# Fourth pass of an FFN's inner products: each matrix's two halves in one load, gate with two tiles and up with three

## The chip, the cores and the metric

The kernel runs on one core of a Trainium2 chip. The metric is the device time of one execution in microseconds, and less is better. Five engines work side by side, each with its own queue of instructions: TensorE (PE, with PEld for weight loads), VectorE (DVE), ScalarE (ACT), GpSimd (POOL) and SyncE (SP), which here issues nearly all DMAs. An instruction waits at the head of its engine's queue until its inputs are there and the buffer that it writes is free; whatever stands behind it on that engine waits too.

## The reference

One block of a network on a sequence of 2048 tokens of width 1024: a mixer of stick-breaking attention and causal pooling, and then a dense feed-forward part, which is where the change lies:

```python
h = rmsnorm(x, g_ffn_pre[l]) * (1.0 + scale_f) + shift_f
f = (jax.nn.silu(h @ w_gate[l]) * (h @ w_up[l])) @ w_down[l]
x = x + gate_f * rmsnorm(f, g_ffn_post[l])
```

`w_gate` and `w_up` are 1024 x 2816, `w_down` is 2816 x 1024, all in f32.

## The kernel before, in words

The three products of the feed-forward part are done by a fast matrix scheme of seven products instead of eight (Strassen's, in Winograd's form), on two levels. The outer level splits tokens, width and the 22 column blocks of 128 into halves. Some of its products are done first, in four passes, `p1` to `p4`; each pass again uses the seven-product scheme. A pass has 11 columns `j`, a column has seven steps, and a step is two pairs of operands, each multiplied in three matmuls (every f32 operand is split into a high and a low part, and high x high, high x low and low x high are added). After the four passes the main stage begins, whose first column is `gate_up(0)`.

A column of a pass is made by `inner(q, j)`; `m = 11 q + j` counts columns, so the fourth pass is `q == 3`, `m` from 33 to 43. Its parts:

- `load()`: the weights of the column into raw tiles. In passes one to three that is a tile with a 256 KB block of gate and one of up. In the fourth pass the operands are the sums of the two halves of the weights' rows, so four blocks come: `g`, `g2`, `u`, `u2nd`.
- `row_sum` (fourth pass alone): POOL adds `g2` into `g`, and `u2nd` into `u`.
- `s12` and `s34`: POOL makes the scheme's four sums of the blocks of `g` and `u`, in tiles `s`.
- `split_w` in each step: ACT makes the high part and its rounded copy, DVE subtracts for the low part (L1177), into operand tiles `w` for PE. The seven steps take `g`, `s12`, `s12`, `g`, `s34`, `u`, `s34`, and their banks are called `a`, `e`, `f`, `b`, `h`, `i`, `d`; in the trace they are `ap`, `ep` and so on.
- `take_*` and `done`: DVE adds the banks up; a finished partial sum lies in a tile `p_c` of tag `s`, which has six buffers, and is stored by SP to DRAM (`pd`) two steps later. The main stage loads it again (`px`).

The order is set by a list of steps. Each step carries work for earlier steps, with the number of steps ahead:

```python
r[0].ahead = [({1: 9, 2: 12}.get(m, 16 if q == 3 else 14), load), (5 if m == 1 else 8, s12), (4 if m == 1 else 7, s34)]
if q == 3:
    r[0].ahead += [(10, lambda: row_sum("g", "g2")), (9, lambda: row_sum("u", "u2nd"))]
```

So a column's loads are asked for 16 steps ahead, its row sums 10 and 9, `s12` 8 and `s34` 7. On PE, ACT, DVE and POOL the instructions run in this order. SP's queue is ordered by a scheduler that places each DMA by when it reckons its tile free and its data ready; that order is fixed at build time.

Between the steps POOL also adds up the token operands of later products: `hs` tiles, loaded by SP (L1617) from DRAM and added by POOL (L1687).

Raw tiles come from two pools, `fx` and `ring`, each with one buffer per tag: `w320` and `w321` in either, and `gf` in `fx`; all hold two blocks of 256 KB (`cu`, of two buffers, holds one block each). The fourth pass before: the first halves of gate and up in one tile, which goes around three places (`fx` `w321`, `ring` `w320`, `fx` `w320`); the second halves of both in another, which goes around two (`ring` `w321`, `gf`).

Of the kernel before, what the change touches and what calls it, by code (L numbers as in the profile page):

```python
# [17 lines left out]
P = 128  # L18
# [3 lines left out]
HK = KC // 2  # L22
# [6 lines left out]
TB = 512  # L29
# [10 lines left out]
NQ = 4  # L40
# [7 lines left out]
def block_kernel(ctx, tc, x, c, w_cond, b_cond, g_mix_pre, g_mix_post, w_in, w_pool,  # L48
                 pool_scale, w_out, g_ffn_pre, g_ffn_post, w_gate, w_up, w_down, out):
    nc = tc.nc  # L50
# [3 lines left out]
    w_gate, w_up, w_down = w_gate[0], w_up[0], w_down[0]  # L54
# [10 lines left out]
    def rows(w):  # L65
        return w.rearrange("(kc p) n -> p kc n", p=P)

    def mm3(ps, terms, first=True, last=True):

        n = len(terms)  # L70
        for i, ((lh, ll), (rh, rl)) in enumerate(terms):
            nc.tensor.matmul(ps, lh, rh, start=first and i == 0, stop=False)  # L72
            nc.tensor.matmul(ps, lh, rl, start=False, stop=False)  # L73
            nc.tensor.matmul(ps, ll, rh, start=False, stop=last and i == n - 1)  # L74

    def open_pool(stack, name, bufs=1, side=None):
        kw = {"side": side} if side else {}
        return stack.enter_context(tc.tile_pool(name=name, bufs=bufs, reuse_waits="tile", **kw))
# [39 lines left out]
    def ft(tag, name, shape=(P, TB)):  # L118
        return fx.tile(list(shape), F32, tag=tag, bufs=FT[tag], name=name)
# [980 lines left out]
    for n in range(len(steps) + OFF):  # L1100
# [4 lines left out]
        if n < len(steps):  # L1105
            u, i = steps[n]
# [6 lines left out]
        if n >= OFF:  # L1113
            u, b = steps[n - OFF]
# [37 lines left out]
    ring = open_pool(ctx, "ring", bufs=RB)  # L1152
    SBT = S // 2
    NTS = SBT // P
    HF = NF // 2
# [3 lines left out]
    def operand(name, pool=None):  # L1159
        if pool is None:  # L1160
            used[0] += 1
            pool = fx if fx is not None and used[0] % (RB + 1) == 0 else ring
        return [pool.tile([P, TB], F32R, tag=f"w{n}", bufs=1 if pool is fx else RB, name=f"{name}_{n}") for n in "hl"]

    def split_by_bank(hi, lo, src):

        if low_ps is None:
            return split(hi, lo, src)
        nc.scalar.copy(hi, src)
        n = 1  # L1170
        for d in src.shape[1:]:
            n *= d
        both = low_ps("rounded")[:, 0:n]
        if len(src.shape) == 3:
            both = both.rearrange("p (a b) -> p a b", a=src.shape[1])
        nc.scalar.copy(both, raw(hi))
        nc.vector.tensor_tensor(lo, src, both, ALU.subtract)  # L1177
# [123 lines left out]
    def raw_tile(pool, n, name, shape):  # L1301
        tag = f"w32{int(n)}"
        return ft(tag, f"{name}_32{int(n)}", shape) if pool is fx else pool.tile(list(shape), F32, tag=tag, bufs=1, name=f"{name}_32{int(n)}")

    def raw_pair(pool, name, shape):
        return [raw_tile(pool, n, name, shape) for n in range(2)]

    def later(steps_on, do):
        takes.setdefault(n + steps_on, []).append(do)

    def rows_of(src, k0, f):
        return rows(src)[:, k0:k0 + HK, f * P:(f + 1) * P]

    def inner(q, j):

        p = f"p{q + 1}"
        name = f"{p}_{j}"
        m = HF * q + j
        st = {}

        def load():
            if m == 0:
                st["g"], st["u"], st["s12"], st["s34"] = (t[:, n] for t in raw_pair(ring, name, (P, 2, TB)) for n in range(2))
            else:
                turn = 0 if m == 1 else (31 - m) % 4
                pool, n = ((fx, 1), (ring, 0), (fx, 0))[m % 3] if m >= 30 else (ring if turn > 1 else fx, turn % 2 == 0)
                w = ft("gf", f"{name}_32", (P, 2, TB)) if m == NQ * HF - 1 else raw_tile(pool, n, name, (P, 2, TB))
                st["g"], st["u"] = w[:, 0], w[:, 1]
            k0, f = ((0, j), (HK, j), (HK, j + HF), (0, j + HF))[q]
            parts = [("g", w_gate, k0), ("u", w_up, k0)]  # L1330
            if q == 3:
                if m == NQ * HF - 2:
                    st["g2"], st["u2nd"] = (ft("cu", f"{name}_2{n}") for n in "gu")
                else:
                    w = raw_tile(ring, 1, f"{name}_2", (P, 2, TB)) if m % 2 else ft("gf", f"{name}_2", (P, 2, TB))
                    st["g2"], st["u2nd"] = w[:, 0], w[:, 1]
                parts = [parts[0], ("g2", w_gate, HK), parts[1], ("u2nd", w_up, HK)]
            for n, src, k in parts:
                (nc.scalar if m in (4, 5) else nc.sync).dma_start(st[n].rearrange("p (k n) -> p k n", k=HK), rows_of(src, k, f))

        def row_sum(n, other):
            nc.gpsimd.tensor_tensor(st[n], st[n], st[other], ALU.add)

        half = TB // 2
        one, two = slice(0, half), slice(half, TB)

        def sum_tile(n):
            if n not in st:
                st[n] = ft("sr", f"{name}_{n}")
            return st[n]  # L1350

        def s12():
            t, g, u = sum_tile("s12"), st["g"], st["u"]
            nc.gpsimd.tensor_tensor(t[:, one], u[:, one], u[:, two], ALU.add)
            nc.gpsimd.tensor_tensor(t[:, two], t[:, one], g[:, one], ALU.subtract)

        def s34():
            t, g, u = sum_tile("s34"), st["g"], st["u"]
            nc.gpsimd.tensor_tensor(t[:, one], g[:, one], u[:, one], ALU.subtract)
            nc.gpsimd.tensor_tensor(t[:, two], g[:, two], st["s12"][:, two], ALU.subtract)  # L1360

        def step(w, part, v, vpart, bank, after, split_first=True):

            def split_w():
                if split_first:
                    pair = operand(f"{name}_{w}")
                    cols = two if w == "u" else slice(0, TB)
                    split_by_bank(*(t[:, cols] for t in pair), st[w][:, cols])
                    st[w + "r"] = [x.rearrange("p (k n) -> p k n", k=HK) for x in pair]

            def mm():
                st[bank] = (e_ps if bank in "de" else p_ps)(f"{bank}{name}")
                (wh, wl), (th, tl) = st[w + "r"], ys[p][v]
                mm3(st[bank], [((wh[:, 2 * part + k, :], wl[:, 2 * part + k, :]), (th[:, 2 * vpart + k, :], tl[:, 2 * vpart + k, :]))
                               for k in range(2)])

            return Step(1, split_w, mm, [(1, do) for do in after])

        def keep(kind, sb, t):
            nc.sync.dma_start(pd[sb][:, j, q // 2 * 4 + 2 * kind + q % 2, :], t)  # L1380

        def done(kind, sb, ps, rest):
            t = ft("s", f"{name}_c{kind}{sb}")
            nc.vector.tensor_tensor(t, ps, rest, ALU.add)
            later(2, lambda: keep(kind, sb, t))

        def take_p1():
            st["p1"] = ft("p1", f"p1{name}")
            nc.scalar.copy(st["p1"], st["a"])

        def take_p5():
            st["u4"] = t = ft("gf" if not q and m and m % 2 == 0 else "u4", f"u4{name}")
            if not q:
                nc.scalar.copy(t, st["e"])

        def take_p6():
            st["u2"] = ft("u2", f"u2{name}")
            nc.vector.tensor_tensor(st["u2"], st["f"], st["p1"], ALU.add)
            if q:
                nc.vector.tensor_tensor(st["u4"], st["e"], st["u2"], ALU.add)  # L1400
            else:
                nc.gpsimd.tensor_tensor(st["u4"], st["u4"], st["u2"], ALU.add)

        def take_p7():
            st["u3"] = ft("u3", f"u3{name}")
            nc.vector.tensor_tensor(st["u3"], st["h"], st["u2"], ALU.add)

        r = [step("g", 0, "ya", 0, "a", [take_p1]),
             step("s12", 0, "v14", 0, "e", [take_p5]),
             step("s12", 1, "v32", 1, "f", [take_p6], False),  # L1410
             step("g", 1, "ya", 1, "b", [lambda: done(0, 0, st["b"], st["p1"])], False),
             step("s34", 0, "v32", 0, "h", [take_p7, lambda: done(1, 1, st["e"], st["u3"])]),
             step("u", 1, "v14", 1, "i", [lambda: done(1, 0, st["i"], st["u3"])]),
             step("s34", 1, "y22", 0, "d", [lambda: done(0, 1, st["d"], st["u4"])], False)]
# [3 lines that stand above are left out]
        return r  # L1418
# [747 lines left out]
```

## Time and profile before

| what | us |
|---|---|
| median of three runs | 2224.97 |
| the runs | 2221.27, 2224.97, 2226.73 |
| the profiled execution, its time | 2223.88 |
| its span | 2222.1 |
| PE busy | 2179.7 |
| second pass, from the first matmul of its `ap` to that of the third | 105.76 |
| third pass, first eight columns | 76.16 |
| fourth pass, first ten columns (1305.64 to 1420.32) | 114.68 |

All views are of the profiled execution, and times in them are microseconds from its span's start. In the tables by stretch a cell is an engine's busy time and, after the x, its instructions. In a table of waits a row says which engine, at which line, waited for whom. In a timeline a row has its start, its length, engine, line, operation, `out<-in` by tile names without numbers, and in square brackets the idle time ahead of it with what ended it. All loads of the passes are called `p` in the trace (`p_s` the sums, `p_g_l`, `p_u_l`, `p_s_l` low parts).

### The profile page before, as it was taken

To read this page: it belongs to the slowest core of one execution; us is meant where nothing else is said; L and a number is where in the kernel's file an instruction comes from. 1 tells how busy PE (TensorE), PEld (TensorE's weight loads), DVE (VectorE), ACT (ScalarE), POOL (GpSimd) and SP (SyncE) were. 2 spreads that over 40 slices of the span, in tenths; PEclk is the share of its full clock that TensorE was granted. 3 is DMA by queue.
4 is the path that set the end of the run, shared out by engine and by line. 5 is a ranking of instruction groups with operands and counts; after the bars stand their busy time and mean duration, and the time that the engine had idled before them with its cause. 6 is when DMAs were issued, how large, how long until landed. Compare 5 with 4: busy or idle time off the path is not lost.

```text
span 2222.1 us, 34293 instructions
## 1 busy us (share of the span) xinstructions
PE 2179.7 (98%) x10349; PEld 1794.8 (81%) x10349; DVE 1673.5 (75%) x2552; ACT 1355.9 (61%) x2796; POOL 1215.6 (55%) x1700
## 2 busy tenths in 40 slices
PE   8999999999999999999999999899999999999998
PEld 6888888888888888878888877678888888888887
DVE  7874599999999966557777867697788775577566
ACT  5434599989889845447666655554444444455444
POOL 1452277787779965547888666556565520033003
PEclk9999999999999999999999999999999999999999
DMA  8996876534444456678899867899999897679553
GB/s 312 343 291 205 286 208 179 157 96 119 130 114 110 133 176 209 199 230 286 272 318 334 265 204 247 271 316 314 324 320 296 294 338 269 208 243 329 183 199 121
DMA packets 365909, 524.78 MB, mean 236 GB/s; under 512 B 24534, under 2 KB 204314, under 8 KB 358172
## 3 DMA queue, kind: packets, MB, share of 16 engines
q1 hardware_dynamic: 363164, 521.02, 71.7%
q8 instruction: 82, 1.34, 0.3%
q10 hardware_dynamic: 2560, 1.58, 0.2%
q14 instruction: 103, 0.84, 0.1%
HBM read 350.01 MB, written 172.49 MB: 235 GB/s over the span
## 4 chain that ended last, share of the span: by engine, by line
PE 77%; DVE 6%; DMA 5%; POOL 4%; issue 3%; ACT 3%; SPq 1%; DVEq 0%; POOLq 0%; ACTq 0%
PE wt L964 4%; PE dn0p L73 3%; PE dn0p L74 3%; PE dn0p L72 3%; PE dn1p L72 3%; PE dn1p L73 3%; PE dn1p L74 3%; PE av L980 2%; PE z L929 2%; PE z L930 2%; PE av L979 2%; DMA pd<-p_c 2%; PE mix L72 2%; PE mix L74 2%; PE mix L73 2%
## 5 line engine op out<-in xcount | busy, mean ns | idle before, releaser
L953 POOL TENSOR_TENSOR w<-sg,pr 128x512 f32<-128x512 f32 (+2 forms) x320 | 306.3, 957 | 46.4 <-DVE pr L948 14.7
L948 DVE TENSOR_TENSOR_SCAN pr<-pr,carry,begin 128x512 f32<-128x512 f32 x192 | 244.1, 1271 | 0.0
L932 ACT ACTIVATE sg<-z 128x512 f32<-128x512 f32 (+2 forms) x320 | 183.7, 574 | 50.9 <-PE z L930 40.2
L63 DVE TENSOR_TENSOR wtl<-wt,wth 128x512 fp32r<-128x512 f32 (+1 forms) x320 | 189.7, 593 | 17.8 <-ACT wth L62 15.6
L62 ACT CAST wth<-wt 128x512 fp32r<-128x512 f32 (+1 forms) x320 | 183.1, 572 | 10.4 <-PE wt L964 10.4
L934 ACT ACTIVATE pr<-z 128x512 f32<-128x512 f32 (+2 forms) x320 | 183.1, 572 | 0.0
L964 PE MATMUL wt<-ident,w 128*128 128x128 f32 x1088 | 172.3, 273 | 1.6 <-POOL pr L944 1.1
L964 PEld LDWEIGHTS wt<-ident,w 128*128 128x128 f32 x1088 | 134.1, 140 | 32.7 <-POOL pr L944 1.9
L1481 ACT ACTIVATE sa<-sa 128x512 f32<-128x512 f32 x88 | 54.7, 632 | 154.3 <-DVE sa L1480 147.4
L979 PE MATMUL av<-wth,vt 128*128 128x512 f32 (+1 forms) x320 | 126.2, 394 | 0.9 <-ACT o L984 0.8
L72 PE MATMUL dn0p<-w0p_h,g0p_h 128*128 128x512 f32 x308 | 119.8, 389 | 0.0
L73 PE MATMUL dn0p<-w0p_l,g0p_h 128*128 128x512 f32 x308 | 119.8, 389 | 0.0
L74 PE MATMUL dn0p<-w0p_h,g0p_l 128*128 128x512 f32 x308 | 119.8, 389 | 0.0
L929 PE MATMUL z<-kt,qt 128*128 128x512 f32 (+2 forms) x320 | 118.7, 371 | 0.7 <-ACT pr L934 0.6
L980 PE MATMUL av<-wtl,vt 128*128 128x512 f32 (+1 forms) x320 | 117.7, 368 | 1.3 <-DVE wtl L63 1.2
L63 DVE TENSOR_TENSOR g0p_l<-g0p,g0p_h 128x512 fp32r<-128x512 f32 x77 | 58.4, 759 | 79.5 <-ACT g0p_h L62 79.5
L930 PE MATMUL z<-kt,qt 128*128 128x512 f32 (+2 forms) x320 | 116.9, 365 | 0.0
L72 PE MATMUL dn1p<-w1p_h,g1p_h 128*128 128x512 f32 x292 | 113.6, 389 | 0.0
L73 PE MATMUL dn1p<-w1p_l,g1p_h 128*128 128x512 f32 x292 | 113.6, 389 | 0.0
L74 PE MATMUL dn1p<-w1p_h,g1p_l 128*128 128x512 f32 x292 | 113.6, 389 | 0.0
L945 DVE TENSOR_TENSOR_SCAN pr<-pr,zero,begin 128x128 f32<-128x128 f32 (+3 forms) x128 | 111.3, 871 | 1.7 <-ACT pr L934 1.7
L62 ACT CAST g0p_h<-g0p 128x512 fp32r<-128x512 f32 x77 | 48.0, 623 | 104.9 <-PE dn0p L73 90.9
(847 smaller groups left out, 7157.5 us busy)
## 6 DMA issues: line engine op xcount, KB each, us to landing
pd<-p_c SPq DMA_DIRECT2D x176, 256.0 KB, 4.9
px<-pd SPq DMA_DIRECT2D x42, 1024.0 KB, 8.6
hs<-h2d SPq DMA_DIRECT2D x78, 256.0 KB, 4.7
wc<-in_w_cond_dram SPq DMA_DIRECT2D x32, 512.0 KB, 7.6
qt<-qd SPq DMA_DIRECT2D x64, 256.0 KB, 4.1
p<-in_w_gate_dram SPq DMA_DIRECT2D x52, 256.0 KB, 4.9
p<-in_w_up_dram SPq DMA_DIRECT2D x52, 256.0 KB, 4.9
kt<-kd SPq DMA_DIRECT2D x96, 128.0 KB, 3.3
```

The costliest lines, as they stand in the source:

```text
L62: nc.scalar.copy(hi, src)
L63: low.tensor_tensor(lo, src, raw(hi), ALU.subtract)
L72: nc.tensor.matmul(ps, lh, rh, start=first and i == 0, stop=False)
L73: nc.tensor.matmul(ps, lh, rl, start=False, stop=False)
L74: nc.tensor.matmul(ps, ll, rh, start=False, stop=last and i == n - 1)
L929: nc.tensor.matmul(z[:, 0:L], qt[:, 0, i * P:(i + 1) * P], keys, start=True, stop=False)
L932: nc.scalar.activation(sg[:, 0:L], z[:, 0:L], AF.Sigmoid, scale=0.125)
L934: nc.scalar.activation(pr[:, 0:L], z[:, 0:L], AF.Sigmoid, scale=-0.125)
L948: nc.vector.tensor_tensor_scan(keys, keys, begin, carry, ALU.mult, ALU.bypass)
L953: nc.gpsimd.tensor_tensor(w[:, 0:L], sg[:, 0:L], pr[:, 1:L + 1], ALU.mult)
L964: nc.tensor.transpose(wt[:, i * P:(i + 1) * P], wss[u][i][:, b * P:(b + 1) * P], ident)
L979: nc.tensor.matmul(av[:, lo0:], vb, wh[:, lo0:], start=first, stop=False)
```

## The change

In the fourth pass both halves of one matrix come in one transfer of 512 KB into one tile, `[P, 2, TB]` with the first half in `[:, 0]`: up into the tile that held the first halves (three places), gate into the one that held the second halves (two places; odd columns `m` now in `gf`, even ones in `ring` `w321`). The last column, whose up goes into `gf`, has its gate in two `cu` tiles with two loads of 256 KB; before, two `cu` tiles were used in the column ahead of it. Up's load is asked for after gate's in the code. Row sums, differences, splits and matmuls are as before, and PE, ACT, DVE and POOL have the same instructions in the same order, apart from the tiles' names. SP has 21 DMAs fewer. The diff:

```diff
-            k0, f = ((0, j), (HK, j), (HK, j + HF), (0, j + HF))[q]
-            parts = [("g", w_gate, k0), ("u", w_up, k0)]
             if q == 3:
-                if m == NQ * HF - 2:
-                    st["g2"], st["u2nd"] = (ft("cu", f"{name}_2{n}") for n in "gu")
+                f = j + HF
+                if m == NQ * HF - 1:
+                    st["g"], st["g2"] = (ft("cu", f"{name}_{n}") for n in ("g", "g2"))
+                    for n, k in (("g", 0), ("g2", HK)):
+                        nc.sync.dma_start(st[n].rearrange("p (k n) -> p k n", k=HK), rows_of(w_gate, k, f))
                 else:
-                    w = raw_tile(ring, 1, f"{name}_2", (P, 2, TB)) if m % 2 else ft("gf", f"{name}_2", (P, 2, TB))
-                    st["g2"], st["u2nd"] = w[:, 0], w[:, 1]
-                parts = [parts[0], ("g2", w_gate, HK), parts[1], ("u2nd", w_up, HK)]
-            for n, src, k in parts:
-                (nc.scalar if m in (4, 5) else nc.sync).dma_start(st[n].rearrange("p (k n) -> p k n", k=HK), rows_of(src, k, f))
+                    v = ft("gf", f"{name}_g", (P, 2, TB)) if m % 2 else raw_tile(ring, 1, f"{name}_g", (P, 2, TB))
+                    st["g"], st["g2"] = v[:, 0], v[:, 1]
+                    nc.sync.dma_start(v.rearrange("p h (k n) -> p (h k) n", k=HK), rows(w_gate)[:, :, f * P:(f + 1) * P])
+                st["u"], st["u2nd"] = w[:, 0], w[:, 1]
+                nc.sync.dma_start(w.rearrange("p h (k n) -> p (h k) n", k=HK), rows(w_up)[:, :, f * P:(f + 1) * P])
+                return
+            k0, f = ((0, j), (HK, j), (HK, j + HF))[q]
+            for n, src in (("g", w_gate), ("u", w_up)):
+                (nc.scalar if m in (4, 5) else nc.sync).dma_start(st[n].rearrange("p (k n) -> p k n", k=HK), rows_of(src, k0, f))
```

SP's queue before, in the middle of the fourth pass. A name such as `p4_5_2` is pass 4, column 5, second halves; `p4_4_320` the first halves of column 4; `c00`, `c11`, `c10`, `c01` are a column's four partial sums:

```order
L1339 DMA p4_5_2_17376<-in_w_gate_dram 128x4x128
L1380 DMA pd0_158<-p4_0_c00_17138 128x512
L1339 DMA p4_5_2_17376<-in_w_up_dram 128x4x128
L1380 DMA pd1_159<-p4_0_c11_17152 128x512
L1380 DMA pd0_158<-p4_0_c10_17166 128x512
L1339 DMA p4_4_320_17248<-in_w_gate_dram 128x4x128
L1339 DMA p4_4_320_17248<-in_w_up_dram 128x4x128
L1617 DMA hs0_2_1_17338<-h2d6_126 128x512
L1380 DMA pd1_159<-p4_0_c01_17207 128x512
L1617 DMA hs0_2_3_17340<-h2d6_126 128x512
```

The same place after (lines are five further on):

```order
L1385 DMA pd0_158<-p4_0_c00_17130 128x512
L1385 DMA pd1_159<-p4_0_c11_17144 128x512
L1385 DMA pd0_158<-p4_0_c10_17158 128x512
L1340 DMA p4_4_320_17240<-in_w_up_dram 128x8x128
L1622 DMA hs0_2_1_17328<-h2d6_126 128x512
L1385 DMA pd1_159<-p4_0_c01_17199 128x512
L1338 DMA p4_4_g_17241<-in_w_gate_dram 128x8x128
L1622 DMA hs0_2_3_17330<-h2d6_126 128x512
L1385 DMA pd0_158<-p4_1_c00_17251 128x512
```

Before, the second halves of a column stood ahead of the first halves of the column before it; now a column's two loads stand together, after three and after four stores, and no load of a later column is ahead of them.

SP's queue before at the end of the pass, from the last loads of the pass to the main stage's first, `g_0`:

```order
L1339 DMA p4_9_321_17860<-in_w_up_dram 128x4x128
L1339 DMA p4_10_32_17979<-in_w_up_dram 128x4x128
L1339 DMA p4_10_2_321_17980<-in_w_up_dram 128x4x128
L1617 DMA hs8_0_1_18367<-h2d12_132 128x512
L1380 DMA pd0_158<-p4_6_c00_17874 128x512
L1617 DMA hs8_3_1_18097<-h2d15_135 128x512
L1380 DMA pd1_159<-p4_6_c11_17889 128x512
L1380 DMA pd0_158<-p4_6_c10_17906 128x512
L1617 DMA hs8_3_3_18099<-h2d15_135 128x512
L1440 DMA g_0_321_18013<-in_w_gate_dram 128x8x128
```

The same place after, from the stores of column 6 on:

```order
L1385 DMA pd0_158<-p4_6_c00_17853 128x512
L1385 DMA pd1_159<-p4_6_c11_17868 128x512
L1385 DMA pd0_158<-p4_6_c10_17885 128x512
L1622 DMA hs8_3_1_18076<-h2d15_135 128x512
L1622 DMA hs8_3_3_18078<-h2d15_135 128x512
L1445 DMA g_0_320_18010<-in_w_gate_dram 128x8x128
L1385 DMA pd1_159<-p4_6_c01_17923 128x512
L1340 DMA p4_10_32_17958<-in_w_up_dram 128x8x128
L1622 DMA hs8_0_1_18346<-h2d12_132 128x512
L1385 DMA pd0_158<-p4_7_c00_17971 128x512
```

The last column's up has moved behind a load of the main stage, `g_0_320`, and `g_0_321` has moved behind the stores of column 7.

## The prediction

> **What bounds the kernel now.** I read the page first: busy times, then the slices.
>
> ```profile
> span 2222.1 us, 34293 instructions
> PE 2179.7 (98%) x10349; PEld 1794.8 (81%) x10349; DVE 1673.5 (75%) x2552; ACT 1355.9 (61%) x2796; POOL 1215.6 (55%) x1700
> PE   8999999999999999999999999899999999999998
> DMA  8996876534444456678899867899999897679553
> ```
>
> TensorE (PE) is the bound, and only its pauses can be won. Most slices read 9. The one 8 inside the row is slice 26 of 40, near 1390 us, where the fourth pass runs. So the second view is a table of stretches, cut where a first matmul of a row `ap` starts: the second pass, the first eight columns of the third pass, its last three, ten columns of the fourth, its last column, and the first column of the main stage.
>
> ```profile
> core 0: us, PE busy (x) PEld busy (x) DVE busy (x) ACT busy (x) POOL busy (x), PEclk, DMA share, GB/s
> 1092.12:1197.88 105.76, 105.27 (x463) 86.57 (x462) 82.63 (x137) 68.61 (x131) 90.92 (x100) 1.00 0.93 313
> 1197.88:1274.04 76.16, 76.16 (x337) 63.08 (x336) 60.00 (x99) 50.90 (x98) 52.34 (x59) 1.00 0.84 277
> 1274.04:1305.64 31.60, 29.64 (x128) 23.34 (x126) 23.44 (x40) 17.54 (x34) 21.21 (x25) 1.00 0.73 245
> 1305.64:1420.32 114.68, 101.47 (x422) 78.17 (x420) 74.44 (x124) 62.78 (x118) 74.32 (x76) 0.99 0.71 226
> 1420.32:1431.99 11.67, 10.26 (x43) 7.49 (x42) 7.26 (x13) 4.69 (x9) 3.23 (x3) 1.00 0.82 270
> 1431.99:1468.25 36.26, 34.89 (x150) 28.08 (x151) 30.00 (x45) 23.53 (x41) 19.68 (x16) 1.00 0.99 345
> ```
>
> A column j is 42 matmuls (7 steps of 6). The second row shows eight columns in 76.16 us, PE never idle: 9.52 us each, at full clock. Ten columns of the fourth pass take 114.68 where that rate gives 95.2: 19.48 us lost, 1.95 a column. The stretch before loses 31.60 - 28.56 = 3.04, the last column 11.67 - 9.52 = 2.15. No other engine is full there: DVE works 7.44 us a column, POOL 7.43, ACT 6.28, and the DMA share, 0.71, is lower than in either pass before. So something waits in a ring. The waits of the ten columns, by engine:
>
> ```profile
> PE ep L72 <- DVE p_c L1384: 5.6, 4, 2.7
> PE ap L72 <- DVE u2p L1398: 4.2, 5, 1.9
> DVE p_c L1384 <- DMA pd<-p_c: 33.4, 13, 5.2
> ACT rounded L1176 <- DVE p_s_l L1177: 25.5, 9, 5.4
> SPq L1339 <- POOL p L1342: 32.8, 6, 7.0
> SPq L1617 <- POOL hs L1687: 14.2, 5, 6.1
> ```
>
> (us in total, times, longest.) Read backwards: PE waits for DVE, DVE for stores of partial sums (`pd`) to land so that a slot of `s` is free, and the stores stand in SP's queue, which is held 32.8 us at the loads of L1339 by POOL's row sums, L1342. Order of time shows it closing:
>
> ```profile
> 1317.94 1.29 POOL L1342 TENSOR_TENSOR p<-p,p 128x512 f32<-128x512 f32 x1 [1.30 <-DMA p<-in_w_up_dram]
> 1319.26 0.38 SPq L1339 DMA_DIRECT2D p<-in_w_gate_dram  x1
> 1323.78 0.58 SPq L1339 DMA_DIRECT2D p<-in_w_up_dram  x1
> 1327.44 1.27 POOL L1342 TENSOR_TENSOR p<-p,p 128x512 f32<-128x512 f32 x1 [2.69 <-DMA p<-in_w_gate_dram]
> 1328.87 1.29 POOL L1342 TENSOR_TENSOR p<-p,p 128x512 f32<-128x512 f32 x1 [0.16 <-DVE u2p L1398]
> 1330.19 0.38 SPq L1339 DMA_DIRECT2D p<-in_w_gate_dram  x1
> 1333.40 1.31 SPq L1339 DMA_DIRECT2D p<-in_w_up_dram  x1
> 1340.01 1.30 POOL L1342 TENSOR_TENSOR p<-p,p 128x512 f32<-128x512 f32 x1 [0.85 <-DMA p<-in_w_up_dram]
> 1341.33 0.38 SPq L1339 DMA_DIRECT2D p<-in_w_gate_dram  x1
> 1346.02 0.69 DVE L1384 TENSOR_TENSOR p_c<-ip,u3p 128x512 f32<-128x512 f32 x1 [2.67 <-DMA pd<-p_c]
> ```
>
> Up's row sum of a column ends at 1319.23; within 0.03 us SP issues the second-half load of the column two later, which needs the tile that this sum has just read. Behind it in the queue stand stores and, last, the first-half load (1323.78) that the next column's row sums need. It lands, the sums run (1327.44, 1328.87), and SP is let go again at 1330.19, then at 1341.33. One turn is 10.93 and 11.14 us, and gives one column, where PE needs 9.52. At 1346.02 DVE pays: its slot's store left SP only after 1341.33.
>
> **The change part by part.**
>
> *Taken away: the second-half tile that a row sum frees late.* A second half lived in a tile of two buffers; its load for column j+2 waited for the row sum of j, ahead of column j+1's first halves. Afterwards the row sum reads and writes inside one tile; nothing is freed at its end. That wait, 32.8 us on SP, has no instruction to hang on.
>
> *Added: the gate tile of two buffers.* It is freed by DVE's rest of the gate (L1177) and by the second difference `s34` (L1360), both of column j, and its load for j+2 waits for both. So a ring remains, but it gives two columns a turn and has 19.04 us for them. From `s34` to `s34`: issue 0.38, landing L, two row sums, two halves of `s12`, one head-sum (`hs`, L1687) between, two of `s34`. Durations and landings:
>
> ```profile
> 1330.24 0.73 POOL L1354 TENSOR_TENSOR p_s<-p 128x256 f32<-128x256 f32 x1
> 1344.30 1.28 POOL L1687 TENSOR_TENSOR hs<-hs,hs 128x512 f32<-128x512 f32 x1
> L1339 SPq DMA_DIRECT2D p<-in_w_up_dram x19: 425/491/1315, 1289.7 to 1394.9; - x19
> DMA to landing us min/median/max: 3.1/4.6/5.8
> ...
> L1440 SPq DMA_DIRECT2D g<-in_w_gate_dram x22: 383/384/3434, 1407.6 to 1728.8; - x22
> DMA to landing us min/median/max: 6.3/8.4/10.8
> ```
>
> That is 0.38 + L + 2.58 + 1.46 + 1.28 + 1.46 = L + 7.2. No load of 512 KB runs in this pass; bounds: L is at least the 4.6 us of a 256 KB load here, and at most the 10.8 us of a 512 KB load in the main stage. I take 8.4, the same size. The turn is then 15.6 us against 19.04, 3.4 to spare; with 10.8 it is 18.0 and still fits. Price 0, range 0 to 0. The cover is this slack; without it the next late thing is POOL's row sum and behind it the same p_c.
>
> The Trainium skill (DMA: Bandwidth & Descriptors, section Anatomy of one DMA) fits 2.0 us plus bytes over 436 GB/s, on GpSimd's path; for 512 KB an estimate of 3.2 us by that page. By it the turn would be 10.4 us and the sum below the same, with no chance left for the slow ring; the trace's 8.4 for that size says otherwise and is used.
>
> *Up's tile of three buffers* is freed by DVE a whole column earlier than needed; price 0, covered by that column's 9.52 us.
>
> *Loads merged: 4 issues a column become 2*, 21 fewer on SP. At 0.38 to 0.49 us each a column's SP work falls by about 0.9 us. SP is not full, so it is worth 0 to 9 us (ten columns), and I count it inside the ring above: 0.
>
> *Moved in SP's queue:* the gate load now stands behind a column's fourth store and ahead of two `hs` loads and the next column's stores. It passes no instruction on POOL, DVE, ACT or PE. While it waits for `s34` (POOL runs that one column ahead of PE), stores behind it are late. Price per column: between the second pass, where loads of both kinds share SP and a column loses (105.76 - 104.72)/11 = 0.09 us, and the stretch before the ring fills, 3.04/3 = 1.01. Ten columns: 0.9 to 10.1. POOL here has 7.43 us of work a column, less than the second pass's 8.27, and the DMA share is lower too, so I stay near the lower end: 3.3, about half of it the `hs` waits at L1617, which the change leaves.
>
> *The end of the pass.* The last column's gate goes into two tiles of another kind with two loads, and of the main stage's first loads one, `g_0_321`, moves behind five stores and one `hs` load. Price between -2.15 (its loss goes) and +2.72 (two steps more of PE); I take +0.5.
>
> *The stretch 1274 to 1305.* Its waits begin with an `hs` on POOL, which stays, and end in the ring: of 3.04 I take back 0.7.
>
> Sum: -(19.48 - 3.3) + 0.5 - 0.7 = -16.4 us, on the profiled execution's 2223.88: **2207.5, said as 2208**. That execution lies 1.1 us under the median of the three runs, 2224.97, which range over 5.5 us; about 0.3% (6.7 us) is what a measurement of this kernel can tell from no change.
>
> **The rivals.**
>
> *B, the pass at PE's rate.* The third pass shows that seven steps, their stores and `hs` loads fit when loads come in time. Both small terms vanish: 19.48 + 3.04 + 2.15 = 24.7, so 2199. Against: DVE must finish `u2p` just in time for `ap` (4.2 us in five waits), which is no load's fault.
>
> *C, the new place of the gate load holds SP.* If each gate load stands behind one `hs` wait of the longest kind, 6.1, the ring is 15.6 + 6.1 = 21.7 us for two columns, 10.85 each: ten columns in 108.5, a gain of 6.2, and 2217.7. At the mean, 14.2/5 = 2.8, it is 18.4 and costs nothing. I give half the gain lost, 2212 to 2218.
>
> *D, no real change.* PE's waits name DVE, none names a load. If DVE's chain rather than its stores set the pace, time stays 2224. Against: 33.4 us of DVE's idleness ends with a landing of `pd`.
>
> *E, slower: the ring of two columns turns too slowly.* It decides once L + 7.2 is over 22.94 (two columns of now), L over 15.8. With L = 20, ten columns take 136 us: +21, 2245. For it: 512 KB take nearly twice the time of 256 KB, and one buffer fewer stands behind gate. Against: no 512 KB load of the two tiles in the main stage took over 10.8, at a DMA share of 0.99.
>
> The Trainium skill (Perfetto Trace Analysis, section DMA Optimizations) says that where DMA engines are generally idle, splitting a transfer may let the work end sooner; the change merges instead, with the share at 0.71. By that rule E's case gains; that the row sum starts only when both halves are there, merged or not, speaks against it.
>
> **How the numbers follow.** A, as summed, 2204 to 2212: 0.60. B, 2199 to 2204: 0.14. C, 2212 to 2218: 0.15. D: 0.06. E: 0.05. The range takes A, B and most of C, 2200 to 2217. Faster than 2218.3: A, B and most of C, 0.84; within 0.3%: the rest of C and D, 0.10; slower, over 2231.6: E and a little of D, 0.06.
>
> **What would show it.** Right: SP's wait for POOL L1342 at the loads is gone; DVE's wait for `pd` in the fourth pass falls from 33.4 us to under 8; ten columns take 97 to 100 us; the DMA share there rises towards 0.82 with the same bytes. Ten columns under 97 with a last column over 12 shows the last term. Wrong: SP held at the gate loads by `s34` or `hs` for over 20 us (C, then E); gate loads landing in over 12 us (E); DVE idle before `u2p` or ACT's casts with SP free (D).

## The result, and the profile after

The changed kernel takes 2202.97 us (median of four runs, 2201.41 to 2204.54) against 2225.45 before (2221.27 to 2226.73): a ratio of 0.9902, interval 0.9885 to 0.9919, some 22 us or 1% faster. The profiled execution took 2203.83 us, with a span of 2202.0.

The page's first lines and PE's row of slices after; the 8 of the twenty-sixth slice is gone:

```profile
span 2202.0 us, 34273 instructions
PE 2172.7 (99%) x10349; PEld 1796.3 (82%) x10349; DVE 1673.7 (76%) x2552; ACT 1356.3 (62%) x2796; POOL 1215.6 (55%) x1700
PE   8999999999999999999999999999999999999998
```

The stretches after, cut at the same instructions as before (third pass's last three columns, ten columns of the fourth, its last, the main stage's first):

```profile
core 0: us, PE busy (x) PEld busy (x) DVE busy (x) ACT busy (x) POOL busy (x), PEclk, DMA share, GB/s
1276.01:1307.71 31.70, 29.64 (x128) 23.35 (x127) 23.47 (x40) 17.58 (x34) 25.00 (x29) 1.00 0.87 296
1307.71:1402.91 95.20, 95.20 (x422) 78.84 (x421) 76.78 (x126) 63.28 (x118) 67.44 (x69) 1.00 0.85 268
1402.91:1414.63 11.72, 10.02 (x43) 7.57 (x42) 5.78 (x11) 4.70 (x9) 7.12 (x7) 1.00 0.59 192
1414.63:1448.74 34.11, 34.10 (x151) 28.25 (x151) 29.78 (x46) 24.25 (x42) 19.20 (x15) 1.00 1.01 358
```

Ten columns take 95.20 us where they took 114.68, and PE is busy through all of it: exactly 9.52 us a column. That is 19.48 us. The stretch ahead of them loses what it lost (31.70, before 31.60), so does the last column (11.72, before 11.67), and the main stage's first column wins 2.15 (36.26 to 34.11). Together -21.48. These stretches began 1.97 us later (1276.01 against 1274.04), from differences further ahead, in passes that the change doesn't touch: 1.1 of it is there at the start of the second pass (1093.22 against 1092.12). A second profile of the same kernel began them at 1274.63.

The waits in the ten columns after, of DVE for stores and the longest of SP:

```profile
DVE p_c L1389 <- DMA pd<-p_c: 2.1, 1, 2.1
SPq L1385 <- DVE p_c L1389: 13.7, 19, 2.6
SPq L1622 <- POOL hs L1692: 13.3, 3, 7.2
SPq L1340 <- DVE p_u_l L1177: 6.0, 6, 2.0
SPq L1338 <- DVE p_g_l L1177: 1.2, 4, 0.5
```

SP's wait for a row sum, 32.8 us before, has no row any more; DVE waits 2.1 us for stores where it waited 33.4. SP's waits for `hs`, 14.2 before, are still 13.3 and cost nothing: 7.2 us at the head of SP's queue pass without a pause on PE. SP's longest wait in total is now for partial sums that aren't made yet (L1385); it costs PE nothing either.

Gate's eight loads of 512 KB in these columns (L1338), from issue to landing:

```profile
L1338 SPq DMA_DIRECT2D p_g<-in_w_gate_dram x8: 383/384/1017, 1303.5 to 1372.7; - x8
...
DMA to landing us min/median/max: 5.6/6.6/7.0
```

Longer than the 4.6 us of a 256 KB load in this pass before, shorter than the 8.4 of the main stage.

### The profile page after: what moved, and what is told of

It reads as the page before. It is cut to its first block, busy times and chain, and to the rows that moved or that the text cites. A ratio compares the mean times of both kernels' runs of the same rounds, so it can differ in the third digit from the quotient of the medians.

```text
span 2202.0 us, 34273 instructions
## 1 busy us (share of the span) xinstructions
PE 2172.7 (99%) x10349; PEld 1796.3 (82%) x10349; DVE 1673.7 (76%) x2552; ACT 1356.3 (62%) x2796; POOL 1215.6 (55%) x1700
## 4 chain that ended last, share of the span: by engine, by line
PE 52%; POOL 2%; DVE 2%; DMA 1%; ACT 1%; issue 1%; SPq 0%; DVEq 0%; POOLq 0%; ACTq 0%
PE dn0p L74 3%; PE dn0p L73 3%; PE dn0p L72 3%; PE dn1p L73 3%; PE dn1p L72 3%; PE dn1p L74 3%; PE t_g L72 2%; PE t_u L72 2%; PE t_g L73 2%; PE t_u L73 2%; PE t_g L74 2%; PE t_u L74 2%; PE mix L72 1%; PE mix L73 1%; PE mix L74 1%
## 5 line engine op out<-in xcount | busy, mean ns | idle before, releaser
L964 PEld LDWEIGHTS wt<-ident,w 128*128 128x128 f32 x1088 | 134.1, 140 | 32.8 <-POOL pr L944 1.9
```

Source lines behind the costliest of these rows:

```text
L964: nc.tensor.transpose(wt[:, i * P:(i + 1) * P], wss[u][i][:, b * P:(b + 1) * P], ident)
```

## The experiments

The change does four things at once: half the loads, twice the size; tiles by matrix instead of by half; another pairing of what shares a place; and, through these, another order in SP's queue. Theory A holds the queue's order to be the cause: SP stood at a load that waited for POOL's row sum, with the first halves behind it that the next row sum needed.

**Four loads in the changed kernel's tiles.**

```diff
-nc.sync.dma_start(v.rearrange("p h (k n) -> p (h k) n", k=HK), rows(w_gate)[:, :, f * P:(f + 1) * P])
+for n, k in (("g", 0), ("g2", HK)):
+    nc.sync.dma_start(st[n].rearrange("p (k n) -> p k n", k=HK), rows_of(w_gate, k, f))
```

and likewise for up.

> The changed kernel's tiles, but each 512 KB load as two of 256 KB, so four loads a column as before. Theory A (the queue: in the kernel before, SP stood at the second halves' load until the row sum of two columns earlier was done, with the first halves of the next column behind it): the tiles decide, not the size, so 2203 us, at most 2207, ten columns of the fourth pass at 95 to 98 us. Rival B (fewer and larger transfers are the gain: less work for SP, less waiting in the queues): back towards before, 2213 to 2225.

2204.08 us, ratio 0.9903 (0.9888 to 0.9918), ten columns in 95.20:

```profile
1307.23:1402.43 95.20, 95.20 (x422) 78.83 (x420) 76.83 (x126) 63.25 (x118) 68.34 (x70) 1.00 0.84 268
```

Neither the size nor the number of transfers is the gain.

**Second halves issued by ACT, in the kernel before.**

```diff
-(nc.scalar if m in (4, 5) else nc.sync).dma_start(st[n].rearrange("p (k n) -> p k n", k=HK), rows_of(src, k, f))
+(nc.scalar if m in (4, 5) or n in ("g2", "u2nd") else nc.sync).dma_start(st[n].rearrange("p (k n) -> p k n", k=HK), rows_of(src, k, f))
```

> The kernel before with one edit: the loads of the second halves are issued by ACT, not by SP, at the place where the program asks for them, 16 steps ahead. Theory A: the row sum that the load waits for lies 8 steps earlier in the program, ACT waits little, and SP's queue is never held by it: 2203 to 2210, ten columns in 95 to 102 us, SP's wait for POOL's row sum gone. Rivals B and C (size, or the mix in a tile): nothing of that has changed, 2220 to 2228; and if ACT is held instead, PE waits for ACT and it is slower than 2228.

2203.56 us, ratio 0.9903 (0.9888 to 0.9919). The stretch of ten columns, and SP's waits at the pass's loads (L1339) in it that name POOL or DMA:

```profile
1308.24:1403.44 95.20, 95.20 (x421) 78.85 (x420) 77.03 (x126) 63.79 (x119) 71.36 (x72) 1.00 0.82 258
...
SPq L1339 <- DMA p<-in_w_gate_dram: 2.1, 1, 2.1
SPq L1339 <- POOL p_s L1355: 0.4, 1, 0.4
```

The tiles by half, four loads and two places for second halves are as before; the loads that wait for a row sum stand in another queue, and SP's stores and `hs` loads follow each other as before up to the last columns. The whole gain of the ten columns is there.

**The second halves' tile held longer, in the kernel before.**

```diff
+def hold():
+    nc.vector.tensor_tensor(st["u2nd"][:, 0:1], st["u2nd"][:, 0:1], st["g2"][:, 0:1], ALU.add)
...
-r[0].ahead += [(10, lambda: row_sum("g", "g2")), (9, lambda: row_sum("u", "u2nd"))]
+r[0].ahead += [(10, lambda: row_sum("g", "g2")), (9, lambda: row_sum("u", "u2nd"))] + [(8, hold)] * (j < HF - 3)
```

> The kernel before, tiles and loads unchanged, with eight tiny DVE additions (one column of 128 numbers, in the second halves' tile, whose numbers are no longer needed) 8 steps ahead of their column: they keep the second halves' tile taken for longer. The one effect on the order is that SP's scheduler now puts the second halves' load of column j+2 behind the first halves' loads of column j+1. Theory A: only the order in SP's queue mattered, so a tile that comes free later makes the kernel faster, 2203 to 2210, ten columns in 95 to 102 us. Rival C' (the second halves have too few places, their load comes too late): held longer it gets worse, 2226 to 2240. Rival B: 2223 to 2228.

2203.17 us, ratio 0.9897 (0.9881 to 0.9913). DVE does more (eight additions, 0.431 us in the mean), the tile comes free later, and it is as fast as the change:

```profile
L1345 DVE TENSOR_TENSOR p<-p 128x1 f32<-128x1 f32 x8 | 3.4, 431 | 0.0
...
1305.76:1400.96 95.20, 95.20 (x422) 78.85 (x420) 78.85 (x132) 64.46 (x121) 71.84 (x72) 1.00 0.84 261
1400.96:1410.48 9.52, 9.52 (x44) 7.89 (x42) 6.77 (x12) 3.55 (x8) 3.84 (x4) 1.00 0.98 336
```

So the loss was not a lack of places. A tile that the scheduler reckoned free early had its load early in SP's queue, where it held what stood behind.

**Places exchanged, in the kernel before: three for the second halves, two for the first.** The first `w` is the tile of three places, the second that of two:

```diff
+                st["g2"], st["u2nd"] = w[:, 0], w[:, 1]
...
-                    w = raw_tile(ring, 1, f"{name}_2", (P, 2, TB)) if m % 2 else ft("gf", f"{name}_2", (P, 2, TB))
-                    st["g2"], st["u2nd"] = w[:, 0], w[:, 1]
+                    w = raw_tile(ring, 1, f"{name}_1", (P, 2, TB)) if m % 2 else ft("gf", f"{name}_1", (P, 2, TB))
+                    st["g"], st["u"] = w[:, 0], w[:, 1]
```

> The kernel before, tiles by half and four loads, but the second halves go around the three places and the first halves around the two (in the last column the first halves lie in two cu tiles). Theory A: the second halves' load for column j+2 no longer waits for a row sum that is just being made (its place was left by column j-1), so SP isn't held: 2203 to 2210; the first halves' ring, from the low part of up through load, row sum and s12 to the next but one, has little to spare. Rival C (a tile that mixes gate and up is the trouble, whichever half it holds): 2220 to 2230.

2226.45 us, ratio 1.0007 (0.9995 to 1.0018): no gain, and in rival C's range instead of A's. SP's timeline and POOL's row sums show that SP is held as before:

```profile
1367.06 2.55 POOL L1343 TENSOR_TENSOR p<-p,p 128x512 f32<-128x512 f32 x2 [3.36 <-DVE b_0l L1177]
1369.63 0.37 SPq L1340 DMA_DIRECT2D p<-in_w_gate_dram  x1
1373.56 0.94 SPq L1340 DMA_DIRECT2D p<-in_w_gate_dram  x1
1379.28 1.29 POOL L1343 TENSOR_TENSOR p<-p,p 128x512 f32<-128x512 f32 x1 [5.38 <-DMA p<-in_w_gate_dram]
```

The row sums of column 6 end at 1369.61; at 1369.63 SP issues the load of second halves that waited for them, now for column 9 instead of 8. Column 7's first halves follow at 1373.56, and its row sum waits 5.38 us for them. A third place only moved the same load to a later column; it still waited for the sum just being made. The mistake was mine in the expectation: a load whose tile comes free at a row sum was put there, with three places as with two. Where PE lost shows that the hold is not paid at once (three columns, three, four):

```profile
1307.12:1345.32 38.20, 31.92 (x127) 25.31 (x126) 22.83 (x39) 21.06 (x39) 22.53 (x24) 0.91 0.76 241
1345.32:1373.88 28.56, 28.56 (x127) 23.65 (x126) 23.73 (x40) 20.06 (x37) 20.33 (x22) 1.00 0.70 223
1373.88:1427.95 54.07, 43.76 (x169) 33.97 (x168) 29.85 (x50) 22.30 (x42) 31.33 (x33) 0.91 0.67 218
```

The middle three lose nothing, though SP stood 14.6 us at row sums there. In that time the row sums of columns 5, 6 and 7 came 12.5, 11.6 and 12.2 us after those of the column before, slower than PE's 9.52, so the lead that they have on PE shrank. The four columns behind lose 15.99; that they pay for this lead is read from these times and was not tried by itself.

**The same, and the second halves held, 5 steps ahead.**

> The kernel with the places exchanged (three for the second halves, two for the first), which stayed at 2226 us, with the eight tiny DVE additions that keep the second halves' tile taken, here 5 steps ahead. In its trace SP was still held at second halves' loads (14.6 us in three columns), since with three places the load for column j+3 is put where the row sum of j ends, again ahead of the first halves of j+1. The additions put it behind them. Theory A (the order in SP's queue): now 2203 to 2210, ten columns in 95 to 102 us. Rival C (two places are too few for first halves, or the mix in a tile): stays at 2222 to 2230.

2215.04 us, ratio 0.9960 (0.9945 to 0.9975): some two fifths of the gain, between A's range and C's. Its first six columns and the next four:

```profile
1305.98:1363.18 57.20, 57.20 (x254) 47.22 (x252) 48.85 (x85) 41.01 (x76) 38.58 (x39) 1.00 0.80 252
1363.18:1416.11 52.93, 42.73 (x170) 32.60 (x169) 29.16 (x49) 22.31 (x42) 31.88 (x33) 0.94 0.68 216
```

Six columns at 9.53 us, where the unheld kernel lost 9.6 us in the first three alone (38.20 against 28.56). The next four lose 14.85, nearly as much as without the additions (15.99), so something at the end of the pass stops them that the held additions don't reach. SP stands there for 8.2 us at first halves' loads into `cu` tiles, until POOL's head-sums are done, and 6.0 us at a load of the main stage for a row sum; no run tells which of them costs it. The next two runs meet such a hold again.

**Gate in three places and up in two, in the changed kernel.** In all columns but the last:

```diff
 v = ft("gf", f"{name}_g", (P, 2, TB)) if m % 2 else raw_tile(ring, 1, f"{name}_g", (P, 2, TB))
+v, w = w, v
```

> The changed kernel with gate in the three places and up in the two. Theory A: up's place is freed by DVE's low part of up (L1177), 5.2 us later in the turn than the place it has now; in the changed kernel's trace the column's s12 is ready 6.1 us before ACT takes it, so the load that comes 5.2 us later just fits: 2203 to 2212. Rival F (which matrix has three places is what decides, since up is needed longest): 2215 to 2235.

2218.82 us, ratio 0.9977 (0.9967 to 0.9986): outside A's range and in rival F's. But the loss is all at the end:

```profile
1307.75:1374.39 66.64, 66.64 (x296) 55.20 (x294) 54.55 (x90) 48.17 (x89) 46.62 (x48) 1.00 0.79 252
1374.39:1429.54 55.15, 42.96 (x169) 33.22 (x168) 27.82 (x47) 22.37 (x42) 30.79 (x30) 0.91 0.68 206
```

Seven columns at 9.52: two places for up are enough there, as reckoned. The last four, with the pass's last column, lose 17.07. SP and POOL in that stretch (in the trace `p_g` is the tile of two places, here up's):

```profile
1373.97 1.29 POOL L1693 TENSOR_TENSOR hs<-hs,hs 128x512 f32<-128x512 f32 x1
1375.28 0.38 SPq L1334 DMA_DIRECT2D p_g<-in_w_gate_dram  x1
1377.29 0.48 SPq L1341 DMA_DIRECT2D p_g<-in_w_up_dram  x1
1383.98 1.26 POOL L1348 TENSOR_TENSOR p_g<-p_g 128x512 f32<-128x512 f32 x1 [8.72 <-DMA p_g<-in_w_up_dram]
1385.20 1.26 POOL L1693 TENSOR_TENSOR hs<-hs,hs 128x512 f32<-128x512 f32 x1
1386.48 0.38 SPq L1334 DMA_DIRECT2D p_g<-in_w_gate_dram  x1
```

The same shape in another place: a head-sum (POOL's addition of `hs` tiles, some of which lie in the two `cu` buffers) ends at 1375.26, SP issues at 1375.28 the last column's gate load that waited for its `cu` tile, up's load for column 8 is behind it, POOL waits 8.72 us for that up, and its next head-sum, for which the last column's second gate load waits, comes after it.

**The same, with these two loads issued by ACT.**

```diff
 for n, k in (("g", 0), ("g2", HK)):
-    nc.sync.dma_start(st[n].rearrange("p (k n) -> p k n", k=HK), rows_of(w_gate, k, f))
+    nc.scalar.dma_start(st[n].rearrange("p (k n) -> p k n", k=HK), rows_of(w_gate, k, f))
```

> The kernel with gate in three places and up in two, and one edit: the last column's two gate loads (into cu tiles) are issued by ACT. In the trace without the edit the first seven columns take 9.52 us each, and the last four lose 17 us; there SP stands at these two loads for POOL's head-sums (7.3 us at one of them) with up's loads of the columns 8 and 9 behind it, and POOL then waits 14.0 us for these ups. Theory A, in another place: with the two loads out of SP's queue the last columns lose at most 6 us, 2204 to 2211. Rival F (up with two places is late by itself): the loss stays, 2215 to 2221.

2210.64 us, ratio 0.9933 (0.9918 to 0.9948): 8 us back, in A's range and not in F's. The seven columns still take 66.64, the last four 47.69 where they took 55.15; 9.6 us of loss stay, more than the 6 expected, with SP waiting 17.0 us at `hs` loads there and 6.2 at up's. So the hold at the two loads was a good part of it and not all; what the rest is was not tried.

**One place for gate, in the changed kernel.**

```diff
-v = ft("gf", f"{name}_g", (P, 2, TB)) if m % 2 else raw_tile(ring, 1, f"{name}_g", (P, 2, TB))
+v = raw_tile(ring, 1, f"{name}_g", (P, 2, TB))
```

> The changed kernel with one place for gate instead of two (only the ring tile w321). It tests the sum for gate's ring: L + 7.2 us from s34 to s34, with L = 6.7 as gate's loads landed in the changed kernel, is 13.9 us, now for one column instead of two. Ten columns then take 139 where they take 95.2: 2203 + 44 = 2247, between 2240 and 2256. If the ring isn't what I took it for (SP's order alone matters, whatever the number of places), it stays under 2215.

2227.75 us, ratio 1.0016 (1.0006 to 1.0025): slower by 25 than the change, not by 44, and outside both ranges. The ring is there:

```profile
1336.56 0.73 POOL L1365 TENSOR_TENSOR p_s<-p_g,p_s 128x256 f32<-128x256 f32 x1
1337.32 0.38 SPq L1338 DMA_DIRECT2D p_g<-in_w_gate_dram  x1
1341.45 1.30 POOL L1347 TENSOR_TENSOR p_g<-p_g 128x512 f32<-128x512 f32 x1 [1.55 <-DMA p_g<-in_w_gate_dram]
1346.27 0.75 POOL L1365 TENSOR_TENSOR p_s<-p_g,p_s 128x256 f32<-128x256 f32 x1
1348.43 0.38 SPq L1338 DMA_DIRECT2D p_g<-in_w_gate_dram  x1
```

`s34` ends at 1337.29, the load goes at 1337.32, has landed by 1341.45, `s34` of the next column ends at 1347.02. Seven turns from the load at 1312.95 to that at 1400.26 take 12.47 us each, ten columns 122.90. What I had wrong was mainly L: a 512 KB load lands in 4.7 us here (4.0 to 6.1, ten loads), not 6.7, and with 4.7 the sum L + 7.2 gives 11.9, half a microsecond under the 12.47.

**The changed kernel with the last column's gate loads by ACT**, the edit of the run two above.

> The changed kernel with the same edit, the last column's two gate loads issued by ACT. Its last column takes 11.73 us; SP's wait at these loads is 4.7 us in its trace, with up's load for column 9 behind it, but that up has three places and is early. Theory A: at most the 2.2 us of the last column go, 2200.5 to 2203.5; if ACT is held in turn, up to 2207.

> The changed kernel once more, on the same chip as the run with the last gate loads by ACT, so that the two can be compared: 2201 to 2205.

2200.61 us (2197.87 to 2202.12), ratio 0.9886 (0.9871 to 0.9901), beside 2201.95 (2201.27 to 2204.67), ratio 0.9897 (0.9881 to 0.9914), for the changed kernel again. The last column with the edit and without it:

```profile
1401.67:1411.19 9.52, 9.52 (x44) 7.88 (x42) 6.86 (x12) 4.74 (x10) 4.00 (x5) 1.00 0.93 321
...
1400.76:1412.22 11.46, 9.96 (x43) 7.57 (x42) 5.79 (x11) 4.70 (x9) 7.12 (x7) 1.00 0.60 201
```

The last column's pause goes, 1.94 us. In whole executions that is 1.3 us between medians, with intervals that overlap: the trace shows it, the times don't settle it. Its median is the lowest of these runs.

## Why the prediction was right

*The number.* 2202.97 lies in the stated range, under the band of the case that was summed (A, 2204 to 2212) and in that of B (2199 to 2204). Of the signs, SP's wait for the row sums is gone, DVE's wait for stores fell to 2.1 us and the DMA share rose to 0.85; ten columns took 95.20 where 97 to 100 was the sign.

*What bounds.* The ring of row sum, SP's queue, first halves and row sum was what held PE: taking its link out of SP's queue in two other ways (loads by ACT, tile held longer) gave the same 95.20 us. The prediction named the tile that "a row sum frees late" as what is taken away. That word was off: a still later release cured it. The place in the queue was the fault. And the row sums were not the only hold. The ten columns before, the first six and the last four, with SP's longest waits for POOL at the pass's loads in each:

```profile
1305.64:1373.37 67.73, 61.39 (x253) 47.34 (x252) 45.16 (x76) 40.50 (x76) 43.44 (x45) 0.97 0.70 224
SPq L1339 <- POOL p L1342: 32.8, 6, 7.0
...
1373.37:1420.32 46.95, 40.09 (x170) 30.84 (x168) 29.29 (x49) 22.27 (x42) 30.88 (x32) 1.00 0.72 229
SPq L1339 <- POOL hs L1687: 6.3, 2, 4.2
```

All 32.8 us lie in the first six, which lose 10.61. The last four lose 8.87; there SP stood 6.3 us at the second halves of column 9, whose `cu` tiles wait for head-sums. The prediction put the whole 19.48 down to the row sums. Both repairs changed that place too (ACT issues these loads, or SP waits 1.9 us there), so how much of the 8.87 is this hold and how much is lead lost earlier stays open.

*Gate's ring.* L was taken as 8.4; it was 6.6 (5.6 to 7.0), so by the prediction's sum the turn is 13.8 against 19.04 and, as forecast, costs nothing. The run with one place shows that the ring exists and what it costs when it has only one column's time. By the fit in the Trainium skill (DMA: Bandwidth & Descriptors, Anatomy of one DMA), which is for GpSimd's path, 3.2 us is the estimate for 512 KB; SP's gate loads of that size landed in 4.7 to 8.4 us in the median, by stage, in these runs.

*Loads merged.* Counted at 0; with four loads 2204.08 beside 2202.97, so 0 it is. The Trainium skill's rule that splitting may help where DMA engines are idle (Perfetto Trace Analysis, DMA Optimizations) found no case here either: at a share of 0.84 to 0.85, split or not, the ten columns took 95.20 us.

*Moved in SP's queue: the term that failed.* 3.3 us were set aside for new waits of SP, and 0.00 came. It was sized between two stretches that lose 0.09 and 1.01 us a column, so that even its lower bound, 0.9, was too high: those losses were taken as the price of SP's waits, with no chain of waits shown that leads to PE. After the change SP waited 13.3 us at `hs` alone, and none of its waits reached PE, whose table of waits is empty there. Here case B was right for the pass, and A for what lies around it.

*The stretch before the pass:* 0.7 taken back, -0.1 measured. SP's wait for a row sum there, 5.3 us, is gone after the change, and the stretch lost as much all the same; its `hs` wait stayed (5.1 before, 5.8 after). *The last column:* +0.5 forecast, +0.05 measured, and in the run with the last two gate loads on ACT its pause is gone. *The main stage's first column* was not in the sum, and gave 2.15: before, PE paused there 0.46 and 0.91 us for a token operand, `t_1`, and after it doesn't; that is 1.4 of it. All other kernels run here had 34.0 to 34.1 in that place, those with a slow pass too, so it is not the pace of the pass; what it is was not tried.

So -16.4 forecast, and -20.05 measured between the two profiled executions (-22.5 between medians): 3.3 more in the queue's term, 2.15 more in the main stage, 0.45 more in the last column, 0.8 less in the stretch ahead, 1.97 less by the later start, and the remaining half microsecond further on. That the sum came so near is in part luck: a gain of 2.15 in a place that no term names is offset by the 1.97 of a later start. C, with half the gain lost, did not happen in the changed kernel, but its mechanism, SP held for head-sums ahead of a load that a row sum needs, is real: with up in two places the last columns lose 17 us, and 7.5 of it came back when the loads that waited were issued by ACT. D and E are out.

## What to carry to other kernels

When a chain of waits goes from the full engine over stores back to a DMA queue, ask what stands at the head of that queue and what is behind it: a load whose buffer comes free at X, ahead of a load that the next X needs, closes a ring, and its turn is then the pace. A third buffer didn't cure it here, and larger transfers weren't needed; putting the load behind the other, or on another queue, was enough, and even a buffer that is released later did it, since the scheduler orders the queue by release. And count a wait on a DMA queue only where a chain leads from it to the full engine: 13.3 us of waiting at `hs` loads cost the changed kernel nothing.

## What the runs showed of the hardware that I had not expected

A 512 KB load of gate landed in 4.7, 6.6 and 8.4 us in the median (one place for gate, the changed kernel, the main stage before), at DMA shares of 0.67, 0.85 and, in that stage's first column, 0.99. In these three the landing time rose with the share of the stretch, and a row from a fuller stage was too high by a quarter. Size counts beside it: with four loads, at a share of 0.84, gate's loads of 256 KB in the same columns landed in 4.7 us (3.1 to 5.4).
